# An encoder layer on one Trainium2 core: the sample in two blocks of 512 tokens, low weight parts kept in DRAM

## The chip, the cores and the metric

The kernel runs on one core of a Trainium2 chip. Its time is the device time of one execution in microseconds; less is better. The median of the runs stands for a kernel.

## The reference

One layer of a bidirectional hybrid encoder is applied, with the same weights, to a prompt of 512 tokens and to a sample of 1024 tokens, both 1024 channels wide, in float32.

```python
x = layer_norm(x, ln_in_g, ln_in_b)
h = x @ w_in                                   # 1024 -> 2048
c_val, c_gate, r_x, r_gate = split(h)          # 512 each
c = c_val * sigmoid(c_gate)
c = silu(layer_norm(conv31(c)))                # depthwise over tokens, width 31
rec = rg_lru(conv4(r_x), forward) + rg_lru(conv4(r_x), backward)   # gates 64x64, scan over all tokens
x = layer_norm(ALPHA * x + concat(c, rec * gelu(r_gate)) @ w_out)  # LN1
u = conv3(x @ w_up)                            # 1024 -> 5632, depthwise over tokens, width 3
val, gate = split(u)
x = layer_norm(ALPHA * x + (gelu(gate) * val) @ w_down)            # LN2
```

The scan of the recurrence goes over all tokens, once from the left and once from the right; the two convolutions of the sample reach 15 tokens and 1 token over any cut of it.

## The kernel before

**Products.** Every matrix operand is split in a high part (a copy rounded to f32r, line 236, ScalarE) and a low part (operand minus high part, line 197, VectorE or POOL), and a product is three matmuls of line 258: high x high, high x low, low x high. `weight` (lines 464 to 474) loads a raw weight tile of 128x1024 into a staging slot (ST0 to ST2), and `split` (lines 457 to 459) writes both parts into a weight slot. `lo_eng` names the engine of the low part; "any" leaves it to the scheduler, which takes the engine that would end first.

**The order.** All work is recorded as operations with priorities (a lower number goes first) and then put into a fixed order by a list scheduler (`emit`, line 270) with costs per engine. Each engine then runs its instructions in that order. All DMAs are issued from SyncE (SP), in one queue (line 247). Slots in SBUF and PSUM are given away by name; whoever takes a slot waits for its last user.

**The stages.** LN of the prompt; its w_in product; LN and w_in of the sample (its mixer inputs go to DRAM, `mixs_d`); the prompt's mixer (`mixer_p`, line 694), w_out and LN1 (`w_out_ln1`, line 727); the prompt's feed-forward (`ffn_p`, line 792); the sample's mixer (`mixer_s`, line 848), w_out and LN1 in two halves (line 912); the sample's feed-forward (`ffn_s`, line 928). While the prompt's feed-forward runs on TensorE, the sample's mixer, of lower priority, runs on VectorE, ScalarE and POOL, and its mixed channels go through DRAM (`xcat_d`) before w_out.

**The mixer.** For each of four channel blocks: `conv31` (line 629) has 30 taps, each a scalar_tensor_tensor on VectorE (line 206); each direction of the recurrence has `conv4` (three taps), a split, two gate products with sigmoids, `rg_decay` (line 659; exp, tanh and sqrt, each from another table of ScalarE) and `scan` (line 674). In `mixer_s` these are 1024 tokens wide, two directions for each of four blocks.

**The feed-forward.** The hidden width of 2816 is done in 22 pairs of 128 value and 128 gate channels. For a pair, two up tiles (24 matmuls for 512 tokens each, `mtile`, line 517), the width-3 convolution (`ffn_half`), gelu, a product and a split; then down products, in groups of pairs, are added to the residual. `ffn_p` has 512 tokens, three up slots (W0, W1, G3) and two down slots (A2, A3); `weight` there names POOL for the low parts. `ffn_s` has all 1024 tokens for each loaded weight.

**The end.** The last group of `ffn_s` has four pairs; as each of the eight 128-token tiles is complete, `ln2` (line 788) normalises and stores it.

## Time and profile before

| | us |
|---|---|
| runs (3), median | 1667.08 |
| runs, lowest and highest | 1663.58, 1668.41 |
| the profiled execution | 1662.43 |
| its span, first to last instruction | 1660.7 |
| busy: TensorE, VectorE, ScalarE, POOL | 1574.1, 1219.0, 721.0, 401.6 |
| DMA traffic | 152.35 MB, 27.7% of 16 engines |
| mean granted clock of TensorE | 0.979 |

In the profile a line is the line of a helper: 258 is every product, 266 every transpose, 236 every operation of ScalarE, 206 every scalar_tensor_tensor, 197 every two-tensor operation, 247 every DMA. Shapes tell the operations apart: 128x511 is a tap of the feed-forward's convolution, 128x1009 to 128x1023 taps of the sample's mixer, "128x1024 fp32r" a high or low part of a full weight tile.

### The profile page before, as it was taken

To read this page: it belongs to the slowest core of one execution; us is meant where nothing else is said; L and a number is where in the kernel's file an instruction comes from. 1 tells how busy PE (TensorE), PEld (TensorE's weight loads), DVE (VectorE), ACT (ScalarE), POOL (GpSimd) and SP (SyncE) were. 2 spreads that over 40 slices of the span, in tenths; PEclk is the share of its full clock that TensorE was granted. 3 is DMA by queue.
4 is the path that set the end of the run, shared out by engine and by line. 5 is a ranking of instruction groups with operands and counts; after the bars stand their busy time and mean duration, and the time that the engine had idled before them with its cause. 6 is when DMAs were issued, how large, how long until landed. Compare 5 with 4: busy or idle time off the path is not lost.

```text
span 1660.7 us, 17945 instructions
## 1 busy us (share of the span) xinstructions
PE 1574.1 (95%) x7008; PEld 1294.8 (78%) x7008; DVE 1219.0 (73%) x1608; ACT 721.0 (43%) x866; POOL 401.6 (24%) x230
## 2 busy tenths in 40 slices
PE   5999999999999999997899999999999999999995
PEld 5887777887877778776678788888888888888884
DVE  8999996999999998867776575555555555544548
ACT  3636767247957548586432422222232232221321
POOL 3123333136565456664120200000000000000006
PEclk9999999999999989999999999999999999999998
DMA  8632114243233233243742311111111111110102
GB/s 319 205 102 76 64 51 168 86 142 125 89 115 92 72 111 105 76 140 114 264 154 89 101 51 40 49 52 51 50 45 45 38 64 51 38 52 25 39 13 102
DMA packets 45877, 152.35 MB, mean 92 GB/s; under 512 B 5088, under 2 KB 5216, under 8 KB 45664
## 3 DMA queue, kind: packets, MB, share of 16 engines
q1 hardware_dynamic: 45792, 151.21, 27.7%
q8 instruction: 55, 0.90, 0.2%
q14 instruction: 30, 0.25, 0.0%
HBM read 128.12 MB, written 23.07 MB: 91 GB/s over the span
## 4 chain that ended last, share of the span: by engine, by line
PE 47%; DVE 3%; DMA 2%; ACT 1%; issue 1%; POOL 0%; SPq 0%; DVEq 0%; ACTq 0%
PE b L258 46%; DVE b L206 1%; DMA b<-xcat_d 1%; DVE b L197 1%; ACT b L236 1%; PE b L266 0%; DMA xcat_d<-b 0%; POOL b L197 0%; DVE b L413 0%; ACT L236 0%; DMA b<-w_up 0%; SPq L247 0%; DVE b L220 0%; DVE b L415 0%; DVEq L206 0%
## 5 line engine op out<-in xcount | busy, mean ns | idle before, releaser
L258 PE MATMUL b<-b,b 128*128 128x512 f32 (+1 forms) x6720 | 1546.2, 391 | 38.9 <-DVE b L197 20.1
L258 PEld LDWEIGHTS b<-b,b 128*128 128x128 f32 x6720 | 1260.7, 191 | 309.8 <-DVE b L197 28.4
L236 ACT ACTIVATE b<-b 128x1024 fp32r<-128x1024 f32 (+3 forms) x443 | 366.0, 850 | 678.1 <-PE b L258 422.1
L197 DVE TENSOR_TENSOR b<-b,b 128x512 f32<-128x512 f32 (+3 forms) x519 | 443.8, 874 | 264.4 <-ACT b L236 172.0
L206 DVE SCALAR_TENSOR_TENSOR b<-b,b,b 128x511 f32<-128x511 f32 (+20 forms) x668 | 557.8, 852 | 91.5 <-ACT b L236 79.4
L197 POOL TENSOR_TENSOR b<-b,b 128x1024 fp32r<-128x1024 f32 (+3 forms) x176 | 330.9, 1894 | 1157.2 <-DVE b L220 867.4
L236 ACT ACTIVATE b<-b,b 128x512 f32<-128x512 f32 (+2 forms) x330 | 251.4, 782 | 222.1 <-PE b L258 143.3
L236 ACT ACT_TABLE_LOAD x93 | 119.3, 1283 | 19.4 <-DVE b L206 17.2
L206 DVE SCALAR_TENSOR_TENSOR b<-b,b 128x512 f32<-128x512 f32 (+1 forms) x121 | 95.8, 807 | 25.9 <-PE b L258 13.5
L197 POOL TENSOR_TENSOR b<-b 128x512 f32<-128x512 f32 x46 | 70.8, 1543 | 95.2 <-ACT b L236 87.0
L413 DVE BATCH_NORM_STATS2 b<-b 128x6 f32<-128x512 f32 x84 | 57.0, 689 | 20.6 <-PE b L266 15.0
L266 PE MATMUL b<-b,b 128*128 128x128 f32 x288 | 42.2, 289 | 30.5 <-DVE b L206 12.8
L266 PEld LDWEIGHTS b<-b,b 128*128 128x128 f32 x288 | 35.3, 148 | 38.4 <-issue 12.2
L197 DVE TENSOR_TENSOR b<-b 128x1024 f32<-128x1024 f32 (+2 forms) x30 | 32.4, 1081 | 27.7 <-ACT b L236 27.4
L206 DVE SCALAR_TENSOR_TENSOR b<-b 128x1 f32<-128x1 f32 (+2 forms) x59 | 27.8, 474 | 3.5 <-POOL b L197 2.6
L677 DVE TENSOR_TENSOR_SCAN b<-b 128x512 f32<-128x512 f32 (+1 forms) x16 | 28.3, 1768 | 0.3
L220 DVE TENSOR_SCALAR b<-b 128x1 f32<-128x1 f32 (+1 forms) x61 | 10.2, 171 | 1.7
L415 DVE BATCH_NORM_AGGREGATE b<-b 128x2 f32<-128x12 f32 (+1 forms) x48 | 9.6, 199 | 1.0
masks.py:199 POOL TENSOR_SCALAR_AFFINE_SELECT b<-b 128x128 f32<-128x128 f32 x1 | 0.3, 292 | 0.1
L607 DVE RECIPROCAL b<-b 128x8 f32<-128x8 f32 x1 | 0.2, 204 | 0.0
L613 DVE RECIPROCAL b<-b 128x8 f32<-128x8 f32 x1 | 0.2, 203 | 0.0
masks.py:197 POOL MEMSET b<- 128x128 f32 x1 | 0.2, 204 | 0.0
(6 smaller groups left out, 0.6 us busy)
## 6 DMA issues: line engine op xcount, KB each, us to landing
b<-w_up SPq DMA_DIRECT2D x88, 512.0 KB, 3.7
b<-w_in SPq DMA_DIRECT2D x32, 512.0 KB, 3.8
b<-w_out SPq DMA_DIRECT2D x24, 512.0 KB, 4.2
b<-w_down SPq DMA_DIRECT2D x44, 256.0 KB, 3.1
b<-w_down SPq DMA_DIRECT2D x22, 512.0 KB, 3.6
mixs_d<-b SPq DMA_DIRECT2D x12, 512.0 KB, 2.6
b<-mixs_d SPq DMA_DIRECT2D x12, 512.0 KB, 3.5
b<-gb SPq DMA_DIRECT2D x10, 512.0 KB, 6.9
```

The lines of the kernel that those rows point to most:

```text
L197: return self.op(eng, cost if eng == "any" else cost[eng], lambda e=eng: self.engine(e).tensor_tensor(out=out(), in0=a(), in1=b(), op=op), ...
L206: o = self.op("dve", cost, lambda: self.nc.vector.scalar_tensor_tensor(out=out(), in0=a(), scalar=s() if isinstance(s, View) else s, in1=b ...
L220: return self.op(eng, cost, lambda: e.tensor_scalar(out=out(), in0=a(), scalar1=f(s1), scalar2=f(s2), op0=op0, **({"op1": op1} if op1 is n ...
L236: self.nc.scalar.activation(out=out(), in_=a(), func=func, **k)
L258: self.nc.tensor.matmul(out=out(), lhsT=a(), rhs=b(), start=start and i == 0, stop=stop and i == len(pairs) - 1)
L266: self.nc.tensor.transpose(o(), i(), ident())
L413: S.op("dve", c.n * 1.0417 + 69, lambda i=i, c=c: nc.vector.bn_stats(out=sm_[6 * i:6 * i + 6](), in_=c()), [c], [sm_[6 * i:6 * i + 6]], prio)
L415: S.op("dve", 211, lambda: nc.vector.bn_aggr(out=sm_[12:14](), in_=sm_[0:6 * n]().rearrange("p (a b) -> p a b", a=n)), [sm_[0:6 * n]], [sm ...
L607: S.op("dve", 150, lambda: nc.vector.reciprocal(out=d.all(), in_=c.all()), [c.all], [d.all], pr)
L613: S.op("dve", 150, lambda: nc.vector.reciprocal(out=d.all(), in_=c.all()), [c.all], [d.all], pr)
L677: S.op("dve", out.n * 2.0833 + 69, lambda: nc.vector.tensor_tensor_scan(out=out(), data0=a(), data1=b(), initial=0.0, op0=ALU.mult, op1=AL ...
```

## The change

The sample is cut in two blocks of 512 tokens, and the second block (tokens 512 to 1023, `blk` 1) goes first. The new sequence is: mixer of block 1 beside the prompt's feed-forward; w_out (`residual`) and LN1 (`ln1`) of block 1; mixer of block 0 beside the feed-forward of block 1; w_out and LN1 of block 0; feed-forward of block 0.

- The mixer of block 1 runs the forward recurrence over tokens 0 to 511 too (its output is kept in DRAM, `hf_d`) and carries its last state on; the first state of the backward scan is kept in `hbc`. So block 1 has three chains of 512 tokens per channel block, block 0 one. The mixed channels stay in SBUF (`xcf`); `xcat_d` is gone.
- One feed-forward function serves all three passes of 512 tokens. A weight's low part is computed in the prompt's pass, by "any" engine, and stored to DRAM (`lo_d`); the two later passes load raw tile and low part and compute the high part alone. The same holds for w_in and w_out.
- The last down group of a pass (four pairs, `last`) is recorded after the next block's `residual`, and has a later place on TensorE.
- Token 512 needs token 511, which is known only in the last pass: block 1 leaves its first token's hidden value zero; the pass of block 0 computes it (`f5`), multiplies each raw down tile by it on VectorE (`a5`), and a product with a one-column matrix (`E0`) sums it over partitions before the LN2 of tokens 512 to 639.

The core of the diff:

```diff
+    lo_d = {"in": tc.dram_tile([16, 128, 1024], F32, name="lo_in_d"),
+            "out": tc.dram_tile([8, 128, 1024], F32, name="lo_out_d"),
+            "up": tc.dram_tile([2 * NPAIR, 128, 1024], F32, name="lo_up_d"),
+            "down": tc.dram_tile([NPAIR, 128, 1024], F32, name="lo_down_d")}
+    k_lo = {}
+    raw_of = {}
+    def weight(slot, parts, prio, lo_eng="dve", hi_eng="act", st=None):
+        raw_of[id(w)] = t
+        if all((k, m, c.start) in k_lo for k, m, c, _ in pieces):
+            S.copy(hi_eng, w[0], t, prio)
+            for k, m, c, v in pieces:
+                S.load(v.f32, lo_d[k][m][:, c], prio, r=[k_lo[k, m, c.start]])
         else:
-            S.load(t, src, prio)
-        split(w[0], w[1], t, prio, hi_eng, lo_eng)
+            split(w[0], w[1], t, prio, hi_eng, lo_eng)
+            for k, m, c, v in pieces:
+                key = k_lo[k, m, c.start] = Dram()
+                S.dma(lambda k=k, m=m, c=c: lo_d[k][m][:, c], v.f32, v.n * 512, [v], [key], prio + 1)
...
+    def chain(rx, c, hl, d, j, t0, carry, bk, prio):
+        conv4(rx, lambda a, b: c[0, a:b], d, j, 512, prio, t0, N)
+        split(hl[0], hl[1], c[0], prio, lo_eng="pool")
+        rg_gates(c[0], (hl[0], hl[1]), c[1], d, j, bk, prio)
+        rg_decay(c[0], c[1], c[2], c[3], d, j, prio, "pool")
+        if carry is not None:
+            e = slice(0, 1) if d == 0 else slice(511, 512)
+            S.stt(c[0, e], c[1, e], carry, c[0, e], ALU.mult, ALU.add, prio)
+        scan(c[2], c[1], c[0], d, prio)
+    def mixer_s(blk, xslots, PC, PR):
+        t0 = 512 * blk
+        c0, c1 = (497, N) if blk else (0, 527)
+        xcf = [S.buf(n, [4, 512]) for n in xslots]
+        g = S.buf("G1", [2048])
+        acc = S.buf("G2", [4, 512])
+        ch = rot([S.buf(n, [4, 512]) for n in ("A4", "A5", "A7")])
+        hlb = S.buf("A6", [2, 2, 512], f32r)
+        hls = rot([(hlb[i, 0], hlb[i, 1]) for i in range(2)])
+        bk = rot(["M3", "C1"])
+        def conv(j):
+            S.load(g[1024:1024 + c1 - c0], s_d[j][:, c0:c1], PC, r=[k_s[j]])
+            pc = S.buf("C0", [512], psum=True)
+            conv31(lambda a, b: g[1024 + a - c0:1024 + b - c0], lambda a, b: pc[a:b], j, 512, PC, t0, N)
+            S.copy("act", acc[j], pc.all, PC)
+        def rec(j):
+            rn = N if blk else 515
+            S.load(g[0:rn], s_d[4 + j][:, 0:rn], PR, r=[k_s[4 + j]])
+            rx = lambda a, b: g[a:b]
+            if blk:
+                ca = ch()
+                chain(rx, ca, hls(), 0, j, 0, None, bk, PR)
+                S.dma(lambda j=j: hf_d[j], ca[2], 2 ** 18, [ca[2]], [k_hf[j]], PR)
+                cf = ch()
+                chain(rx, cf, hls(), 0, j, 512, ca[2, 511:512], bk, PR)
+                hf = cf[2]
+            else:
+                hf = None
+            cb = ch()
+            chain(rx, cb, hls(), 1, j, t0, None if blk else hbc[j:j + 1], bk, PR)
+            if blk:
+                S.copy("act", hbc[j:j + 1], cb[2, 0:1], PR)
+            else:
+                hf = cb[1]
+                S.load(hf, hf_d[j], PR, r=[k_hf[j]])
+            S.load(cb[3], s_d[8 + j][:, t0:t0 + 512], PR, r=[k_s[8 + j]])
+            S.tt("dve", cb[2], cb[2], hf, ALU.add, PR)
+            S.tt("dve", xcf[1][j], cb[2], cb[3], ALU.mult, PR)
+        for j in range(4):
+            rec(j)
+            conv(j)
+        nb = rot(["M3", "C1"])
+        for tt in range(4):
+            c = slice(tt * 128, (tt + 1) * 128)
+            conv_norm(lambda j: acc[j, c], [(0, 4, acc[:, c])], tt, "c", nb, PR)
+        for j in range(4):
+            b = S.buf(nb(), [512], psum=True)
+            S.transposes([(b[i * 128:(i + 1) * 128], acc[j, i * 128:(i + 1) * 128]) for i in range(4)], b.all, idn.all, PR)
+            S.act(xcf[0][j], b.all, AF.Silu, col(C_CG + j), col(C_CBB + j), PR)
+        return xcf
...
+    def split_block(xcf, prio):
+        xc = quads(["A4", "A5", "A6", "A7"])
+        for q in (1, 0):
+            for a in (slice(0, 2), slice(2, 4)):
+                split(xc[0][q][a], xc[1][q][a], xcf[q][a], prio, lo_eng="any")
+        return xc
+    GROUPS = [[0]] + [list(range(i, i + 3)) for i in range(1, 16, 3)] + [[16, 17], list(range(18, 22))]
...
+        if blk == 0:
+            a5 = S.buf("A4", [1024])
...
+        def up(p):
+            pr = PR + p * 0.01
+            for s in range(2):
+                m = s * NPAIR + p
+                w = weight(ws(), [("up", m, ALLC)], wprio, lo_eng="any")
+                u = ub()
+                mtile(w, x1, u.all, pr)
+                c = lambda k: col(C_FW + 3 * m + k)
+                v = va[p % 2, s]
+                acc = lambda a, b: va[p % 2, s, a:b]
+                S.act(v, u.all, AF.Identity, c(1), col(C_FB + m), ev)
+                S.stt(acc(1, 512), u[0:511], c(0), acc(1, 512), ALU.mult, ALU.add, ev)
+                S.stt(acc(0, 511), u[1:512], c(2), acc(0, 511), ALU.mult, ALU.add, ev)
+                if blk == 1:
+                    S.copy("dve", sv[m], u[0:2], ev)
+                if blk == 0:
+                    S.stt(acc(511, 512), sv[m, 0:1], c(2), acc(511, 512), ALU.mult, ALU.add, ev)
+                    S.stt(ex[p % 2, s:s + 1], u[511:512], c(0), ut[m:m + 1], ALU.mult, ALU.add, ev)
+            S.act(va[p % 2, 1], va[p % 2, 1], AF.Gelu_apprx_tanh, prio=ev)
+            if blk == 0:
+                S.act(ex[p % 2, 1:2], ex[p % 2, 1:2], AF.Gelu_apprx_tanh, prio=ev)
+                S.tt("dve", f5[p:p + 1], ex[p % 2, 0:1], ex[p % 2, 1:2], ALU.mult, ev)
+            r = slice(lo, 512)
+            S.tt("pool" if blk is None else "any", va[p % 2, 0, r], va[p % 2, 0, r], va[p % 2, 1, r], ALU.mult, ev)
+            f = fb[(p // 2) % 2]
+            split(f[p % 2, 0, r], f[p % 2, 1, r], va[p % 2, 0, r], ev, lo_eng="dve")
...
+                    w = weight(wdslot(), [("down", p_, slice(n_ * 512, (n_ + 1) * 512)) for n_, p_ in cs], wprio + 1,
+                               lo_eng="any")
+                    for i, ch_ in enumerate(cs):
+                        wd[ch_] = (w, i)
+                        if blk == 0:
+                            n_, p_ = ch_
+                            raw = raw_of[id(w)].buf[i * 512:(i + 1) * 512]
+                            o = a5[n_ * 512:(n_ + 1) * 512]
+                            if p_ == 0:
+                                S.ts("dve", o, raw, f5[p_:p_ + 1], ALU.mult, prio=wprio)
+                            else:
+                                S.stt(o, raw, f5[p_:p_ + 1], o, ALU.mult, ALU.add, wprio)
...
+            names = rot(["M2", "C0", "C1", "M3", "U3", "U0", "U1", "U2"])
+            nonlocal wdslot
+            wdslot = rot(["A2", "A3", "G2", "A5"])
+            up(NPAIR - 1)
+            get = wds(grp)
+            bank = {}
+            for i in range(2):
+                for nh in range(2):
+                    bank[nh, i] = S.buf(names(), [512], psum=True)
+                    S.mm(bank[nh, i].all, products(get, nh, i, grp[:-1]), True, False, pr)
...
+    WS = ["W0", "W1", "G3"]
+    xcf1 = mixer_s(1, ("T2", "T3"), 32, 31)
+    last_p = ffn(None, x1P, yP, 50.0, 6, 4)
+    xc1 = split_block(xcf1, 33)
+    y1 = [S.buf("T2", [2, D]), S.buf("T3", [2, D])]
+    UB = ["U3", "M2", "C0", "C1", "U0", "U1", "U2", "U3"]
+    residual(1, 1, xc1, y1, 40, UB, rot(WS), pe=50.2105)
+    last_p()
+    gb1a = load_gb("G2", 1, 36)
+    x1a = ln1(y1, gb1a, quads(["B0", "B1", "B2", "B3"]), "s", 37, rot(["M3", "C0"]), ["dve", "act"])
+    gb2a = load_gb("G1", 2, 40)
+    for i in range(4):
+        ln2(page_of(yP[i // 2], i % 2), gb2a, "p", 38, out_p[i * 128:(i + 1) * 128, :], "act")
+    xcf0 = mixer_s(0, ("T0", "T1"), 52, 51)
+    last_1 = ffn(1, x1a, y1, 60.0, 6, 44)
+    xc0 = split_block(xcf0, 53)
+    y0 = [S.buf("T0", [2, D]), S.buf("T1", [2, D])]
+    residual(1, 0, xc0, y0, 56, UB, rot(WS), pe=60.2105)
+    last_1()
+    gb1b = load_gb("G2", 1, 52)
+    x1b = ln1(y0, gb1b, quads(["B0", "B1", "B2", "B3"]), "s", 53, rot(["M3", "C0"]), ["dve", "act"])
+    gb2b = load_gb("G1", 2, 56)
+    for i in range(1, 4):
+        ln2(page_of(y1[i // 2], i % 2), gb2b, "s", 58, out_s[(4 + i) * 128:(5 + i) * 128, :], "act")
+    last_0 = ffn(0, x1b, y0, 70.0, 6, 64)
+    bank, get, grp, products = last_0()
+    E0 = S.buf("A6", [128], f32r)
+    S.op("pool", 200, lambda: nc.gpsimd.memset(E0.all.f32(), 0.0), [], [E0.all], 60)
+    S.op("pool", 100, lambda: nc.gpsimd.memset(E0[0:1].f32(), 1.0), [], [E0[0:1]], 60)
+    a5 = S.slots["A4"]
+    a5s = S.buf("A7", [2, 1024], f32r)
+    split(a5s[0], a5s[1], a5.all, 5)
+    for i in range(4):
+        for nh in range(2):
+            b = bank[nh, i]
+            S.mm(b.all, products(get, nh, i, grp[-1:] if i < 2 else grp), i >= 2, True, 70.21 + 0.01 * i)
+            yv = y0[i // 2][i % 2, nh * 512:(nh + 1) * 512]
+            S.tt("dve", yv, yv, b.all, ALU.add, 6)
+        if i == 1:
+            for nh in range(2):
+                b = S.buf("M2" if nh == 0 else "C0", [512], psum=True)
+                c = slice(nh * 512, (nh + 1) * 512)
+                S.mm(b.all, [(E0.all, a5s[0, c]), (E0.all, a5s[1, c])], True, True, 70.225)
+                yv = y1[0][0, c]
+                S.tt("dve", yv, yv, b.all, ALU.add, 7)
+            ln2(page_of(y1[0], 0), gb2b, "s", 46.9, out_s[512:640, :], "act", "pool")
+        ln2(page_of(y0[i // 2], i % 2), gb2b, "s", 46 + 0.5 * i, out_s[i * 128:(i + 1) * 128, :], "act" if i < 3 else "dve",
+            "pool" if i == 0 else "dve")
```

`conv31` and `conv4` take a first token and the sequence length as well; the old `w_out_ln1` is cut into `residual` and `ln1`; `ffn_p`, `ffn_s` and the old `mixer_s` are gone.

## Rows read from the trace of the kernel before

**Rows 1.** The page's part 1: busy us (share of the span) and instructions by engine

```profile
PE 1574.1 (95%) x7008; PEld 1294.8 (78%) x7008; DVE 1219.0 (73%) x1608; ACT 721.0 (43%) x866; POOL 401.6 (24%) x230
```

**Rows 2.** Windows by stage: length, busy us (instructions) by engine, clock, DMA share, GB/s

```profile
0.00:41.50 41.50, 24.64 (x173) 23.57 (x174) 35.07 (x52) 14.44 (x17) 15.90 (x19) 1.00 0.85 319
124.50:290.50 166.00, 157.28 (x683) 127.63 (x681) 148.84 (x200) 114.69 (x142) 53.52 (x30) 0.97 0.26 90
290.50:373.50 83.00, 83.00 (x383) 68.97 (x382) 78.50 (x85) 28.11 (x34) 19.08 (x11) 1.00 0.34 114
373.50:747.00 373.50, 352.67 (x1502) 285.00 (x1502) 334.27 (x363) 261.44 (x319) 221.25 (x112) 0.97 0.33 103
747.00:954.50 207.50, 184.64 (x813) 149.18 (x813) 144.57 (x203) 88.12 (x109) 48.50 (x33) 0.94 0.44 145
954.50:1618.50 664.00, 664.00 (x2931) 550.00 (x2930) 361.21 (x520) 166.24 (x184) 0.00 (x0) 1.00 0.15 44
```

**Rows 3.** The same windows, products of line 258 alone on TensorE

```profile
124.50:290.50 166.00, 154.76 (x651) 0.97 0.26 90
373.50:747.00 373.50, 351.00 (x1482) 0.97 0.33 103
747.00:954.50 207.50, 173.62 (x705) 0.94 0.44 145
1618.50:1660.00 41.50, 24.89 (x110) 0.83 0.25 102
```

**Rows 4.** Groups by line and shape, VectorE, 373 to 788 us

```profile
L206 DVE SCALAR_TENSOR_TENSOR b<-b,b,b 128x511 f32<-128x511 f32 x88 | 65.7, 747 | 15.0 <-ACT b L236 13.3
L206 DVE SCALAR_TENSOR_TENSOR b<-b,b 128x512 f32<-128x512 f32 x56 | 49.5, 906 | 10.2 <-ACT b L236 8.9 <-POOL b L197 1.1
L197 DVE TENSOR_TENSOR b<-b,b 128x512 fp32r<-128x512 f32 x24 | 23.8, 995 | 4.4 <-ACT b L236 4.4
L206 DVE SCALAR_TENSOR_TENSOR b<-b,b,b 128x1023 f32<-128x1023 f32 x14 | 22.1, 1580 | 0.1
L677 DVE TENSOR_TENSOR_SCAN b<-b 128x1024 f32<-128x1024 f32 x8 | 18.3, 2289 | 0.2
```

**Rows 5.** The same view, VectorE, 290 to 373 us

```profile
L206 DVE SCALAR_TENSOR_TENSOR b<-b,b 128x512 f32<-128x512 f32 x8 | 5.4, 677 | 0.0
L197 DVE TENSOR_TENSOR b<-b,b 128x512 fp32r<-128x512 f32 x8 | 5.2, 685 | 0.0
L206 DVE SCALAR_TENSOR_TENSOR b<-b,b,b 128x1023 f32<-128x1023 f32 x3 | 3.9, 1297 | 0.0
```

**Rows 6.** The same view, whole span: full-width low parts on POOL and VectorE

```profile
L197 POOL TENSOR_TENSOR b<-b,b 128x1024 fp32r<-128x1024 f32 x91 | 229.4, 2528 | 239.5 <-ACT b L236 195.4 <-issue 40.6 <-POOL b L197 2.0
L197 DVE TENSOR_TENSOR b<-b,b 128x1024 fp32r<-128x1024 f32 x121 | 152.0, 1263 | 153.2 <-ACT b L236 152.7
```

**Rows 7.** The same view, ScalarE, 373 to 788 us; then pieces of the chain

```profile
L236 ACT ACT_TABLE_LOAD x59 | 75.7, 1283 | 11.0 <-DVE b L206 10.1
L236 ACT ACTIVATE b<-b 128x1024 fp32r<-128x1024 f32 x63 | 65.7, 1054 | 44.6 <-PE b L258 20.4 <-DMA b<-w_up 14.6 <-issue 7.2
...
781.41 1.28 ACT L236
782.71 1.54 ACT b L236 x3
```

**Rows 8.** The page's part 6: DMA issues, KB, us to landing

```profile
b<-w_up SPq DMA_DIRECT2D x88, 512.0 KB, 3.7
b<-w_down SPq DMA_DIRECT2D x44, 256.0 KB, 3.1
```

**Rows 9.** Timeline of TensorE, 790 to 830 us: start, us, what, [idle before]

```profile
819.63 6.42 PE L258 MATMUL b<-b,b 128*128 128x512 f32 x20 [2.97 <-DVE b L197]
829.76 0.63 PE L258 MATMUL b<-b,b 128*128 128x512 f32 x1 [3.71 <-DVE b L197]
```

**Rows 10.** Groups by line and shape, VectorE, 1600 to 1661 us

```profile
L206 DVE SCALAR_TENSOR_TENSOR b<-b,b,b 128x1024 f32<-128x1024 f32 x8 | 17.2, 2162 | 0.3
```

More of the change, by code (lines that the diff above doesn't have):

```diff
@@ L820, in ffn_p @@
             pr = PR + (grp[-1] + 0.5) * 0.01
             for nh in range(2):
-                for c in range(0, len(chunks), 2):
-                    cs = chunks[c:c + 2]
-                    if cs[0] not in wd and cs[0][0] <= nh:
-                        w = weight(wdslot(), [w_down[p][:, n_ * 512:(n_ + 1) * 512] for n_, p in cs], 5,
-                                   lo_eng="any" if gi == len(groups) - 1 else "pool")
-                        for i, ch_ in enumerate(cs):
-                            wd[ch_] = (w, i)
```

360 lines of the change are left out of this document (118 added, 242 removed).

## Prediction

> **What bounds the kernel now.** I read the page's totals first, then the stretches, then who waits in the bad ones. TensorE is busy 95% of the span of 1660.7 us [rows 1], so the question is what its products cost at best and where more than that was spent. In the long last stretch, the feed-forward pass of the sample, TensorE never stops: 2931 products of 128x512 in 664.0 us, 226.5 ns each, at granted clock 1.00, the 2.4 GHz level [rows 2]. The change keeps every product, so only time above that rate can be won. I take loss of a stretch as its idle time plus the busy time of its products above 226.5 ns each:
> - 124.5 to 290.5 us (prompt mixer): idle 166.0 - 157.28 = 8.7; 651 products should take 147.5 and took 154.8, so 7.3; loss 16 [rows 2, 3].
> - 373.5 to 747 (prompt feed-forward beside the whole sample mixer, stage A below): idle 20.8; 1482 products should take 335.7 and took 351.0; loss 36.
> - 747 to 954.5 (end of the mixer, w_out, LN1 of the sample): idle 22.9; 705 products should take 159.7 and took 173.6; loss 37.
> - 954.5 to 1618.5: none. After it 110 products in 24.89 us put the last product at 1643.4, and 17 us follow, VectorE's backlog and a store [rows 3, 10].
> - At the start some 18 us before the first products run densely [rows 2].
>
> **Why stage A loses.** VectorE is busy 334 of 373.5 us there and POOL 221 [rows 2]. Operations of VectorE are longer beside POOL: the 1023-wide tap takes 1580 ns against 1297 in 290 to 373, where POOL is nearly quiet (19 of 83 us), and the low part of a 512-wide split 995 against 685 [rows 4, 5]. The order is fixed beforehand, mixer work fills every gap of VectorE, so each excess pushes the feed-forward's evictions behind it back, and TensorE waits. The granted clock is 0.97 in the stretch, partly at the 1.2 GHz level after such gaps.
>
> **The change, part by part.**
>
> *Stage A, VectorE.* Out: 82 of the 120 sample conv31 taps lie here, at some 1.28 us (105 us; the quiet price of the 1023-wide tap is 1.30 [rows 5]). Half the tokens at 512 wide need 120 taps of 0.75 us, the price of the 511-wide tap [rows 4]; of these some 63 fit before 373, where 37 wide ones lie now, so 57 x 0.75 = 43 remain: -62. The 8 wide recurrence chains cost some 14.8 us each (three conv4 taps near 1.5, two gate products 0.68, eight half-width steps 0.86, scan 2.29); the new stage has 12 narrow ones of 7.3: -30. Sums and normalisation halve: -8. In: every low part of the prompt's weights, so far named for POOL, becomes "any". What "any" means can be counted now: POOL did 91 full-width low parts, 87 of them explicitly its own, VectorE 121, of which 92 its own; so 29 of 33 free ones went to VectorE [rows 6]. Of 63 weights 55 move, x 1.22 us = +67. Shorter splits beside a quieter POOL: -6. Since records overlap slightly I scale by 0.95: 364 us (373 to 788) - 37 = 327, against some 376 us of products (1584 of the prompt, 72 for gates, a few transposes). POOL falls from 221 to about 70 us (22 products, 12 low parts, 12 decay products at 1.35 to 1.55 us). The excess of VectorE beside POOL, some 27 us (the 42 widest taps 0.16 to 0.30 us each, 24 low parts 0.31, 56 two-operand steps 0.906 - 0.677 = 0.23 [rows 4, 5]), falls with it to a third. I take the loss of stage A from 36 to 14: -22; ends -31 and -6 (VectorE remains packed and nothing tells me that the remaining excess does not sit on TensorE's path).
>
> *ScalarE in stage A.* Its work is 300 us now, of which 59 table loads are 75.7 [rows 7]. Twelve chains instead of eight and the same 22 gelu calls make perhaps 80 loads: 103 us; total some 330 of 410 us. It stays below TensorE's time. A load costs 1283 ns, and a function starts 0.02 us behind it (781.41 + 1.28, next at 782.71) [rows 7]. The Trainium skill ("ScalarE: Activation LUTs", What ACT_TABLE_LOAD costs) gives a switch about 1.38 us more for a drain and advises to batch by table set; this speaks against a mixer cut in blocks. By that price 80 loads would add 110 us, ScalarE would need 440 us and stage A would end some 30 us later, near 1671; the row shows no such drain, so it has 1 chance in 100, inside the late-mixer rival below.
>
> *Stores in stage A.* 66 stores of 512 KB are new in SP's queue. Each waits there for a low part, and the next raw loads are queued behind it, for which ScalarE's copies wait. Those loads need the staging slot that the same low part releases, so the store waits for nothing that SP didn't wait for before: 0, unless VectorE is late (then stage A's upper end, -6).
>
> *124.5 to 290.5.* Sixteen low parts of w_in, 2.5 us each on POOL [rows 6], become loads; 40 of POOL's 53 us vanish beside a VectorE that is busy 149 of 166 [rows 2]. Loss 16 to 12: -4 (0 to -8).
>
> *Start.* Sixteen stores of 512 KB join a stretch that moves 319 GB/s at a DMA share of 0.85 [rows 2]; the later load of w_in waits behind them in SP's order. 8.4 MB at 319 GB/s are 26 us of traffic, most of it due after 41.5, while 16 w_in tiles are being used up. +3 (0 to +8).
>
> *Transitions.* Now one: mixer end, a round trip of the mixed channels through DRAM, w_out, LN1, with gaps such as 2.97 and 3.71 us that end on the split of channels read back [rows 9]. The round trip goes. After: two transitions (A to B, B to C), each with w_out of one block (192 products, 43.5 us) put before the last four down pairs (96 products, 21.7 us), which cover LN1. VectorE's LN1 takes 4 x (two evictions' rest, statistics, two full-width steps, two low parts) = some 24 us from 3 us before w_out's end, with 4 us of latencies and 5 us of the eight last additions ahead of it by priority: about 29 us. Cover: 21.7, plus some 4 us for the third and fourth down weight, which wait for a slot. So idle 4 + 4 and some 4 at the lower clock: 12 each. 37 to 24: -13 (-25 to -5).
>
> *Stages B and C.* The sample's feed-forward runs twice at 512 columns, each weight in 5.4 us of products instead of 10.9. The high part is again ScalarE's, 1.05 us [rows 7]; the low part is a load, in three slots: 10.9 us from a slot's release to its need, against 3.7 us to landing for 512 KB [rows 8]. Per weight 1.05 MB in 5.4 us, 193 GB/s, below the 319 seen [rows 2]. 66 x 1.22 us of low parts leave VectorE; in C 44 multiplications for the boundary token come (0.8 us each, 35 us), at the lowest priority, hidden by TensorE's 359 us, since VectorE has some 130 us else there. B has four chains and half the taps (130 us of VectorE) beside it; by stage A's measure, a third of its mixer, I take +6 (+2 to +12); C +4 (0 to +12). If a cover fails, see the rivals.
>
> *Boundary.* Four products: +1. *Tail.* Five LN2 of tiles instead of seven or eight behind the last weights; VectorE's work there is 42 us now (16 additions, 16 statistics, eight full-width steps at 2.16, small ones [rows 10]); ten, ten and six of them with what the boundary adds are some 27. But TensorE's last products shrink as well, from 126 (29 us) to 64 (14.5 us). Behind the last product VectorE still has about 12 us and a store some 4.5: 17 now, 16 then: -1 (-3 to +3).
>
> **Sum.** -22 - 4 + 3 - 13 + 6 + 4 + 1 - 1 = -26, so a span of 1635. The profiled execution took 1662.4, 1.7 over its span, and the median of the three runs 1667.1 is 6.4 over that span; on the median's side I forecast **1641 us**, with 1629 to 1661 as its own range.
>
> **Rivals.**
> 1. *More is won:* the loss of A falls to 5, that of 124 to 290 to 8, the transitions to 12 together, B costs 2, C and the start nothing, the tail -3: -31 - 8 - 25 + 2 + 1 - 3 = -64, 1603 us. For it: TensorE ran 664 us without a gap when VectorE was at 54% [rows 2]. Against: VectorE at 87% in A.
> 2. *It doesn't do what it says:* low parts on VectorE take what the smaller mixer gave. A 30, transitions 20 + 12, start 3, 124 to 290 -2, rest as above: 0, 1667 us.
> 3. *The mixer of the second block comes late (slower).* It has the lowest priority on VectorE, and each of the 12 chains passes five engines. If its channels are ready more than 21.7 us after the last up product (near 751), the last down pairs have been used up as filler; then LN1 stands bare. Price: A to B 45 instead of 12 (15 waiting, 27 LN1, 3 clock), A 30: +25, 1692 us. For it: the mixer ends now in a stretch where VectorE is at 70% [rows 2], so on the length of its chains, and each chain has ScalarE's table loads in it [rows 7]. Against: three chain buffers, and 327 us of work for 400 us.
> 4. *Low parts land late (slower).* Down weights have two slots; the third of a group can be fetched only after the first is released. If no up product is ready, 3 us are lost in each of 16 such places of B and C: 48, so 1689 us. Against: 3.1 us for 256 KB [rows 8] and up products in hand.
>
> **Chances.** Forecast 0.43, rival 1 0.24, rival 2 0.13, rival 3 0.12, rival 4 0.08. The range reaches from rival 1 to rival 3, 1603 to 1692. A measurement of this kernel tells some 0.3% (5 us) from no change: faster 0.67, within 0.13, slower 0.20.
>
> **What would show it.** In stage A: POOL near 70 us, the taps at their short price, fewer waits for VectorE, a granted clock near 1.00. Between A and B, and B and C: gaps of 8 us or so, w_out's 192 products right behind the last up product; a long gap before w_out is rival 3. In B and C: 226 ns a product; gaps that end on a load of low parts are rival 4. About 310 MB moved. I am wrong if TensorE idles in B or C, or if ScalarE, not VectorE, ends most waits in A.

## The result and the profile after

The changed kernel takes 1618.39 us (median of four runs, 1616.81 to 1619.14) against 1667.74 us for the kernel before beside it (1663.58 to 1669.47): a ratio of 0.9706, 95% interval 0.9686 to 0.9726. It is faster by 49 us. The profiled execution has a span of 1615.0 us, 45.7 less than before. That lies inside the range of 1603 to 1692, but outside the forecast's own 1629 to 1661.

The page's part 1, busy time by engine, of the kernel after (of before: [rows 1]):

```profile
span 1615.0 us, 19015 instructions
PE 1556.7 (96%) x7012; PEld 1281.2 (79%) x7012; DVE 1200.4 (74%) x1867; ACT 820.3 (51%) x1019; POOL 188.1 (12%) x159
```

Windows of after by stage, with the columns of [rows 2]. The stages have other bounds now: 373.5 to 742 is stage A (w_out of block 1 starts at 742.01), 742 to 812 the way from A to B, 812 to 1163 stage B, 1163 to 1229 the way from B to C, then stage C.

```profile
0.00:41.50 41.50, 24.00 (x173) 22.93 (x174) 35.07 (x52) 14.45 (x17) 15.91 (x19) 1.00 0.95 361
124.50:290.50 166.00, 163.99 (x737) 134.99 (x736) 138.09 (x198) 114.65 (x142) 24.23 (x19) 1.00 0.41 140
373.50:742.00 368.50, 354.44 (x1536) 286.91 (x1534) 329.73 (x442) 251.66 (x308) 70.52 (x49) 0.99 0.60 194
742.00:812.00 70.00, 68.92 (x318) 56.93 (x319) 39.45 (x65) 22.24 (x26) 8.99 (x8) 1.00 0.59 196
812.00:1163.00 351.00, 348.10 (x1549) 287.32 (x1548) 266.25 (x433) 182.75 (x222) 19.32 (x24) 1.00 0.66 216
1163.00:1229.00 66.00, 63.84 (x294) 51.91 (x293) 33.88 (x58) 20.98 (x24) 4.45 (x6) 1.00 0.59 193
1229.00:1577.00 348.00, 345.85 (x1520) 284.17 (x1519) 183.48 (x349) 130.34 (x175) 11.81 (x10) 1.00 0.57 190
```

The same windows with the products of line 258 alone, as in [rows 3]:

```profile
124.50:290.50 166.00, 161.96 (x705) 1.00 0.41 140
373.50:742.00 368.50, 352.17 (x1504) 0.99 0.60 194
742.00:812.00 70.00, 66.21 (x286) 1.00 0.59 196
812.00:1163.00 351.00, 345.82 (x1517) 1.00 0.66 216
1163.00:1229.00 66.00, 61.37 (x264) 1.00 0.59 193
1229.00:1577.00 348.00, 345.61 (x1515) 1.00 0.57 190
```

Loss is worked out as in the prediction: idle time plus the products' time above 226.5 ns each. For 124.5 to 290.5 it is 166.0 - 163.99 = 2.0, and 161.96 - 705 x 0.2265 = 2.3, together 4.3.

| stretch | loss before | forecast | loss after |
|---|---|---|---|
| 124.5 to 290.5 | 16 | 12 | 4.3 |
| stage A | 36 | 14 | 25.6 |
| end of the mixer, w_out, LN1 (one before, two after) | 37 | 24 | 2.5 + 3.7 |
| stage B | 0 | 6 | 5.1 |
| stage C | 0 | 4 | 4.6 |
| from the last product to the end | 17 | 16 | 15.9 |

The way from A to B on TensorE (start, us, what, and in brackets the idle time before it with its releaser):

```profile
742.01 46.32 PE L258 MATMUL b<-b,b 128*128 128x512 f32 x203 [0.95 <-DMA b<-lo_out_d]
788.17 1.03 PE L266 MATMUL b<-b,b 128*128 128x128 f32 x8
798.49 1.06 PE L266 MATMUL b<-b,b 128*128 128x128 f32 x8 [0.19 <-DVE b L206]
800.67 8.23 PE L258 MATMUL b<-b,b 128*128 128x512 f32 x35 [0.88 <-DVE b L197]
808.74 1.03 PE L266 MATMUL b<-b,b 128*128 128x128 f32 x8
```

Where the kernel before had two gaps of 3 to 4 us [rows 9] and more like them, the longest here is 0.95. The transposes of LN1 lie between down products, the last of them at 808.74. From 742 to 1615 us the waits of TensorE (total us, times, longest) are as short; besides these two groups there is the 0.95 us on a low part of w_out above, and 0.5 us in two waits of the transposes:

```profile
PE b L258 <- DVE b L197: 5.9, 10, 1.4
PE b L258 <- DMA b<-lo_down_d: 1.7, 2, 1.1
```

VectorE's groups by shape in stage A (instructions | busy us, mean ns | idle before), to be read against [rows 4]:

```profile
L197 DVE TENSOR_TENSOR b<-b,b 128x1024 fp32r<-128x1024 f32 x59 | 74.7, 1277 | 19.6 <-ACT b L236 16.8 <-DMA lo_up_d<-b 2.1 <-DMA b<-w_down 0.3
L197 DVE TENSOR_TENSOR b<-b,b 128x512 f32<-128x512 f32 x63 | 42.1, 680 | 3.2 <-PE b L258 3.2
L206 DVE SCALAR_TENSOR_TENSOR b<-b,b,b 128x512 f32<-128x512 f32 x54 | 41.6, 773 | 1.2 <-ACT b L236 0.5
L206 DVE SCALAR_TENSOR_TENSOR b<-b 128x512 f32<-128x512 f32 x48 | 34.0, 721 | 0.3
```

### The profile page after: what moved, and what is told of

Read it like the earlier page. It is cut to its first block, busy times and chain, and to the rows that moved or that the text cites. A ratio compares the mean times of both kernels' runs of the same rounds, so it can differ in the third digit from the quotient of the medians.

```text
span 1615.0 us, 19015 instructions
## 1 busy us (share of the span) xinstructions
PE 1556.7 (96%) x7012; PEld 1281.2 (79%) x7012; DVE 1200.4 (74%) x1867; ACT 820.3 (51%) x1019; POOL 188.1 (12%) x159
## 4 chain that ended last, share of the span: by engine, by line
PE 50%; DVE 26%; ACT 10%; DMA 9%; issue 4%; SPq 0%; POOL 0%; DVEq 0%; ACTq 0%; POOLq 0%
PE b L258 48%; DVE b L206 15%; DVE b L197 9%; ACT b L236 7%; DMA b<-w_up 6%; ACT L236 3%; PE b L266 1%; DMA b<-mixs_d 1%; DMA b<-w_down 1%; DVE b L708 1%; DMA lo_in_d<-b 1%; DVE b L413 0%; DMA b<-lo_out_d 0%; DMA b<-xp 0%; SPq L247 0%
## 5 line engine op out<-in xcount | busy, mean ns | idle before, releaser
L258 PE MATMUL b<-b,b 128*128 128x512 f32 (+1 forms) x6724 | 1532.1, 389 | 24.5 <-DVE b L197 15.9
L206 DVE SCALAR_TENSOR_TENSOR b<-b,b,b 128x511 f32<-128x511 f32 (+12 forms) x848 | 593.0, 715 | 177.5 <-ACT b L236 156.6
L236 ACT ACTIVATE b<-b 128x1024 fp32r<-128x1024 f32 (+4 forms) x576 | 447.3, 799 | 533.6 <-PE b L258 197.2
L197 DVE TENSOR_TENSOR b<-b,b 128x512 f32<-128x512 f32 (+6 forms) x483 | 396.0, 840 | 122.8 <-ACT b L236 70.4
L236 ACT ACTIVATE b<-b,b 128x512 f32<-128x512 f32 (+1 forms) x337 | 256.9, 784 | 220.9 <-PE b L258 160.3
L197 POOL TENSOR_TENSOR b<-b,b 128x1 f32<-128x1 f32 (+3 forms) x89 | 113.6, 1282 | 674.1 <-DVE b L220 443.7
L236 ACT ACT_TABLE_LOAD x106 | 136.0, 1283 | 26.7 <-DVE b L206 23.9
L206 DVE SCALAR_TENSOR_TENSOR b<-b,b 128x512 f32<-128x512 f32 (+2 forms) x81 | 53.6, 673 | 62.5 <-PE b L258 61.8
L197 DVE TENSOR_TENSOR b<-b 128x512 f32<-128x512 f32 (+3 forms) x80 | 46.5, 600 | 25.8 <-ACT b L236 24.9
L206 DVE SCALAR_TENSOR_TENSOR b<-b 128x512 f32<-128x512 f32 (+1 forms) x110 | 56.0, 518 | 6.8 <-POOL b L197 3.4
L266 PEld LDWEIGHTS b<-b,b 128*128 128x128 f32 x288 | 34.8, 145 | 23.9 <-DVE b L206 10.7
L708 DVE TENSOR_TENSOR_SCAN b<-b 128x512 f32<-128x512 f32 x24 | 29.3, 1223 | 0.7
```

The source lines that it names most:

```text
L197: return self.op(eng, cost if eng == "any" else cost[eng], lambda e=eng: self.engine(e).tensor_tensor(out=out(), in0=a(), in1=b(), op=op), ...
L206: o = self.op("dve", cost, lambda: self.nc.vector.scalar_tensor_tensor(out=out(), in0=a(), scalar=s() if isinstance(s, View) else s, in1=b ...
L236: self.nc.scalar.activation(out=out(), in_=a(), func=func, **k)
L258: self.nc.tensor.matmul(out=out(), lhsT=a(), rhs=b(), start=start and i == 0, stop=stop and i == len(pairs) - 1)
L266: self.nc.tensor.transpose(o(), i(), ident())
L708: S.op("dve", out.n * 2.0833 + 69, lambda: nc.vector.tensor_tensor_scan(out=out(), data0=a(), data1=b(), initial=0.0, op0=ALU.mult, op1=AL ...
```

## The experiments

The order here goes by question. Ratios are to the kernel before, with 95% intervals. "Over after" is the difference of two ratios, times 1665 us; after itself has 0.9706.

**Is it the place of w_out?** e2 records the last down pairs before w_out, in both transitions:

```diff
-    residual(1, 1, xc1, y1, 40, UB, rot(WS), pe=50.2105)
     last_p()
+    residual(1, 1, xc1, y1, 40, UB, rot(WS), pe=50.22)
...
-    residual(1, 0, xc0, y0, 56, UB, rot(WS), pe=60.2105)
     last_1()
+    residual(1, 0, xc0, y0, 56, UB, rot(WS), pe=60.22)
```

> The changed kernel, but w_out of each sample block is put behind the last four down pairs of the pass before, not ahead of them. Theory (the last down pairs cover LN1): in the changed kernel w_out ends near 785.5 and the last transposes of LN1 start at 808.7, with 1.1 us of TensorE idle between; without the cover TensorE stands still for about 20 us in each of the two transitions and restarts at the 1.2 GHz level: +40 to +50 us over the changed kernel, some 1660 to 1668. Rival (the round trip of the mixed channels through DRAM was the cost, and the order doesn't matter): within 5 us of 1618.

1663.03 us, 0.9995 [0.9981, 1.0009]: 48 us over after, the whole gain. TensorE's timeline of e2 at the same place:

```profile
773.47 40.43 PE L258 MATMUL b<-b,b 128*128 128x512 f32 x177 [1.26 <-DVE b L197]
823.47 1.94 PE L266 MATMUL b<-b,b 128*128 128x128 f32 x8 [8.30 <-DVE b L197]
833.23 1.94 PE L266 MATMUL b<-b,b 128*128 128x128 f32 x8 [5.42 <-DVE b L197]
```

With nothing left to multiply, LN1 stands bare: 8.30 and 5.42 us between its transposes. From 742 to 880 us TensorE idles 20.8 us at a granted clock of 0.93, and from 1163 to 1300 us 19.0, also at 0.93. Without this order a kernel with two transitions pays for both; with it both are nearly free.

**Is it w_in's low parts on POOL?** e3 neither stores nor loads those of w_in, so POOL computes them again for the sample; e7 puts them, and nothing else of the change, into the kernel before; e10 keeps in DRAM only those of w_in; e1 keeps none.

```diff
+                if k == "in":
+                    continue
                 key = k_lo[k, m, c.start] = Dram()
```

> The changed kernel, but the sample's w_in tiles have their low parts computed on POOL again, as before the change, and the low parts of w_in are neither stored nor loaded. Theory (operations of VectorE are longer beside POOL, and this is what TensorE lost in 124.5 to 290.5 us): the loss there goes back from 4 to about 16, taps of 509 to 511 from 750 ns to 830 to 930, and the kernel takes +8 to +12 us, 1626 to 1630. Rival (the gain there comes from elsewhere, such as staging slots that come free earlier for other reasons): within 3 us of 1618; if the stores at the start cost, faster by up to 3.

1636.39, 0.9837 [0.9812, 0.9862]: 22 us over after, more than either figure. The stretch of the prompt's mixer in e3, all engines, and then two of VectorE's groups there:

```profile
124.50:290.50 166.00, 152.69 (x665) 123.55 (x664) 150.24 (x198) 112.06 (x140) 52.88 (x31) 0.98 0.22 74
```

```profile
L206 DVE SCALAR_TENSOR_TENSOR b<-b,b 128x512 f32<-128x512 f32 x24 | 24.1, 1022 | 2.2 <-ACT b L236 2.1
L710 DVE TENSOR_TENSOR_SCAN b<-b 128x512 f32<-128x512 f32 x8 | 11.9, 1489 | 0.1
```

In after the same 24 steps take 827 ns and the 8 scans 1223. With 12 long low parts of POOL in the stretch (one in after) VectorE's 198 instructions take 12 us more, and TensorE lost 13.3 us of idle time in place of 2.0, at clock 0.98. It does 665 instructions there in place of 737, 72 less (16 us at 226.5 ns each), and from 373.5 to 742 us 1506 in place of 1536 (7 us); that makes up the 22. Of the 13.3 us, 7.5 end on VectorE, 3.1 on ScalarE and 2.7 on POOL's own low parts (in after 2.0, all on VectorE). So e3 shows that low parts on POOL cost this time, but not that VectorE's longer operations are the only way.

The edit of e7 (the stores go to a tensor of sixteen tiles, as in the change; its declaration, `weight`'s new argument `m_in` and the three calls that pass it are left out here):

```diff
...
-        split(w[0], w[1], t, prio, hi_eng, lo_eng)
+        if m_in in k_lo:
+            S.copy(hi_eng, w[0], t, prio)
+            S.load(w[1].f32, lo_d[m_in], prio, r=[k_lo[m_in]])
+        else:
+            split(w[0], w[1], t, prio, hi_eng, lo_eng)
+            if m_in is not None:
+                key = k_lo[m_in] = Dram()
+                S.dma(lambda m=m_in: lo_d[m], w[1].f32, w[1].n * 512, [w[1]], [key], prio + 1)
...
```

> The kernel before with one part of the change alone: the low parts of w_in are stored to DRAM by the prompt and loaded by the sample; all else as before. Theory (POOL's 40 us beside VectorE cost the loss of 124.5 to 290.5): the loss there goes from 16 to about 5, and the kernel takes 8 to 12 us less, 1655 to 1659. Rival (the later stages wait for something else anyway, or the stores cost at the start): within 3 us of 1667.

1658.04, 0.9955 [0.9933, 0.9976]: 7.5 us won, where e3 priced the same loads at 22. Windows of e7, with the bounds of [rows 2]:

```profile
124.50:290.50 166.00, 162.32 (x728) 133.18 (x727) 158.00 (x216) 115.98 (x144) 25.06 (x19) 1.00 0.40 136
373.50:747.00 373.50, 339.98 (x1448) 272.85 (x1447) 333.67 (x345) 261.83 (x316) 212.43 (x108) 0.97 0.31 99
747.00:954.50 207.50, 190.16 (x848) 153.98 (x847) 148.29 (x210) 90.89 (x114) 47.23 (x31) 0.96 0.43 145
```

Against [rows 2] TensorE does 728 instructions instead of 683 in the first stretch, and 1448 instead of 1502 in stage A: 45 gained, 54 given back. What comes earlier into an unchanged stage A, with POOL at 212 us, is lost there again. From 747 to 954.5 us it does 848 in place of 813, and these 35 are where e7 comes out ahead.

The edit of e10 is that of e3 with the condition turned round (`k != "in"`).

> The changed kernel with low parts in DRAM for w_in alone; those of w_out, up and down tiles are computed in every pass by 'any' engine. Undoing w_in alone cost 22 us and undoing all 23, so theory: low parts of the feed-forward in DRAM are worth about nothing (0 to 3 us), 1616 to 1622, although VectorE in stage B is near 99% busy. The theory from before the runs (a packed VectorE loses 15 to 20 us in B): 1633 to 1640. If the stores in stage A cost: faster than 1618 by up to 5.

1620.45, 0.9724 [0.9699, 0.9749]: 3 us over after, within the noise. So the low parts of w_up, w_down and w_out in DRAM, 74 of the 90 tiles that are stored, bring 0 to 3 us. Windows of e10:

```profile
373.50:742.00 368.50, 358.60 (x1558) 291.33 (x1557) 334.08 (x443) 248.88 (x306) 72.61 (x50) 0.99 0.34 108
812.00:1163.00 351.00, 344.56 (x1519) 280.96 (x1518) 318.83 (x478) 181.61 (x220) 47.19 (x27) 1.00 0.37 119
```

Without the stores stage A is 22 instructions of TensorE ahead of after (some 5 us), and stage B, where VectorE computes them again and is busy 319 of 351 us, 30 behind (some 7). VectorE at 91% leaves TensorE 6.4 us idle there in place of 2.9, so most of that work is off TensorE's path.

The edit of e1:

```diff
-                key = k_lo[k, m, c.start] = Dram()
-                S.dma(lambda k=k, m=m, c=c: lo_d[k][m][:, c], v.f32, v.n * 512, [v], [key], prio + 1)
+                pass
```

> The changed kernel without low parts in DRAM: every pass computes them ('any' engine in the feed-forward and w_out, POOL in the sample's w_in), nothing is stored or loaded. Theory: VectorE gets some 80 us more in each of stages B and C; B (266 us busy of 351) becomes as packed as stage A and loses 15 to 20 us, C (183 of 348) up to 5, and 124.5 to 290.5 loses its 10 as well: 1645 to 1655. Rival (the doubled DMA traffic and SP's longer queue cost as much as VectorE gains): within 5 us of 1618, with a lower loss in stage A since 66 stores are gone.

1637.85, 0.9847 [0.9815, 0.9879]: 23 us over after, no more than e3 alone. What costs is w_in, not the feed-forward's 66 weights.

**Is it "any" in place of POOL?** e4 names POOL for the low parts of the prompt's feed-forward, as before; e6 gives "any" to the kernel before.

```diff
-                    w = weight(ws(), [("up", m, ALLC)], wprio, lo_eng="any")
+                    w = weight(ws(), [("up", m, ALLC)], wprio, lo_eng="pool" if blk is None else "any")
...
-                               lo_eng="any")
+                               lo_eng="pool" if blk is None and grp[-1] < NPAIR - 1 else "any")
```

> The changed kernel, but in the prompt's pass POOL is named for the low parts of the weights, as before the change ('any' had put nearly all on VectorE). VectorE is rid of some 70 us in stage A, POOL has some 150 us more. Theory (what counts is VectorE's lengthening beside POOL): the loss of stage A goes up from 26 to 30 to 36, so 1622 to 1628. Rival (what counts is how much VectorE has to do): the loss falls to about 15, so 1607 to 1610.

1638.04, 0.9843 [0.982, 0.9867]: 23 us over after; the direction is that of the lengthening theory, the size more than twice its figure. From e4, 373.5 to 725 us: all engines, then TensorE's costliest waits in stage A, then five of VectorE's groups.

```profile
373.50:725.00 351.50, 316.77 (x1354) 255.89 (x1354) 297.19 (x362) 234.56 (x287) 195.39 (x99) 0.96 0.57 182
```

```profile
PE b L258 <- DVE b L206: 23.8, 3, 9.8
```

```profile
L206 DVE SCALAR_TENSOR_TENSOR b<-b 128x512 f32<-128x512 f32 x48 | 53.0, 1116 | 3.6 <-ACT b L236 3.5
L197 DVE TENSOR_TENSOR b<-b,b 128x512 f32<-128x512 f32 x56 | 38.7, 700 | 11.8 <-PE b L258 11.0 <-ACT b L236 0.6
L708 DVE TENSOR_TENSOR_SCAN b<-b 128x512 f32<-128x512 f32 x12 | 20.0, 1665 | 0.2
L206 DVE SCALAR_TENSOR_TENSOR b<-b,b,b 128x510 f32<-128x510 f32 x10 | 14.7, 1474 | 0.2
L206 DVE SCALAR_TENSOR_TENSOR b<-b,b,b 128x507 f32<-128x507 f32 x3 | 2.2, 748 | 0.1
```

VectorE has less to do than in after (297 against 320 us) and TensorE does 111 instructions less. The steps of the recurrence chains (the x48 group) went from 721 to 1116 ns and the scans from 1222 to 1665, but the additions that empty a bank of PSUM only from 680 to 700: an operation with one input in PSUM hardly notices POOL. The taps say the same: widths 497 to 508 belong to `conv31` alone, whose sum lies in a bank of PSUM (`pc`), and keep 731 to 748 ns, while the group of 510, which holds `conv4`'s taps with both inputs in SBUF as well, means 1474. The Trainium skill (GPSIMD Engine Reference, Specifications) says that POOL shares its SBUF interfaces with VectorE and contends with its operations that have two SBUF inputs; the rows agree, and give the sizes.

How it reaches TensorE is the line of 23.8 us: three waits, 9.8 us the longest, on line 206. Here is the first of them in TensorE's timeline, and then VectorE's groups in the 11 us before its end (424.5 to 435.85):

```profile
435.99 23.98 PE L258 MATMUL b<-b,b 128*128 128x512 f32 x96 [6.84 <-DVE b L206]
```

```profile
L206 DVE SCALAR_TENSOR_TENSOR b<-b,b,b 128x511 f32<-128x511 f32 x5 | 3.7, 744 | 0.1
L206 DVE SCALAR_TENSOR_TENSOR b<-b,b,b 128x510 f32<-128x510 f32 x1 | 2.8, 2833 | 0.0
L206 DVE SCALAR_TENSOR_TENSOR b<-b 128x512 f32<-128x512 f32 x2 | 2.4, 1200 | 0.0
```

The last two instructions that end before the wait does, and so before each of the three, are 511 wide: by their place the two taps of the feed-forward's own convolution, which read an up product out of its bank. VectorE was never idle; it had mixer work ahead of them in its fixed order, among it a tap of 0.75 us that took 2.83. So a mixer operation that POOL holds up delays a bank that TensorE needs, though the mixer's results are needed only much later. The sizes fit: in the 30 us before the three waits end, VectorE never pauses for 0.1 us, and its steps, taps and scans take 6.7, 6.9 and 9.1 us more than at their quiet prices (an estimate, with 0.72 us for what is 512 wide, 0.75 for the narrower taps and 1.22 for a scan), beside waits of 6.84, 7.17 and 9.82. What is not shown apart is the order: an edit of this kind makes the scheduler set another one, and in e7, with POOL as busy as before (212 against 221 us), such waits on line 206 in stage A are 14.9 us in four, against 2.8 in one in the kernel before.

The edit of e6, in the kernel before:

```diff
-                w = weight(ws(), w_up[m], 4, lo_eng="pool")
+                w = weight(ws(), w_up[m], 4, lo_eng="any")
...
-                           lo_eng="any" if gi == len(groups) - 1 else "pool")
+                           lo_eng="any")
```

> The kernel before with one part of the change alone: low parts of the prompt's feed-forward weights on 'any' engine instead of POOL. VectorE gets some 67 us more in stage A (364 busy of 415 before), POOL some 150 less. Theory of load: the mixer ends later, so +10 to +25 us, 1677 to 1692. Theory of lengthening (VectorE's operations become shorter beside a quiet POOL, and low parts are ready sooner): within 5 us of 1667, or faster by up to 10.

1683.44, 1.0107 [1.0092, 1.0122]: 18 us slower than before. Windows of e6:

```profile
373.50:747.00 373.50, 365.25 (x1584) 296.60 (x1583) 364.46 (x400) 276.56 (x330) 77.78 (x52) 1.00 0.34 107
747.00:954.50 207.50, 155.10 (x664) 121.33 (x664) 154.80 (x218) 74.18 (x97) 47.86 (x34) 0.84 0.38 130
```

Stage A is nearly cured (1584 instructions against 1502, clock 1.00), with VectorE full (364 of 373.5); the mixer of 1024 tokens is then not done, and behind it 149 instructions are missing. So the same edit costs 18 us with the large mixer and is worth 23 with the smaller one. This is the third rival's mechanism.

**The cut without its two helpers.** e9 takes e1 and e2 together: two blocks, with "any" in the prompt's pass as in the change, but no low parts in DRAM and no covered LN1.

> What is left of the change when both its helpers are undone: the sample in two blocks, but no low parts in DRAM (each pass computes them) and w_out of a block behind the last down pairs. If the two effects seen so far, +48 us for the order and +23 us for the low parts, simply add: 1685 to 1692, so 1.1 to 1.5% slower than the kernel before. If they overlap (a later mixer or a more packed VectorE hides in the bare LN1): 1665 to 1680.

1681.69, 1.0091 [1.0063, 1.012]: slower than before, 64 us over after, where e1 and e2 give 23 + 48 = 71. The cut wins nothing by itself, even with "any" beside it. It makes room for "any" and lets a w_out have products behind it. The cut with POOL named as before was not run.

**What keeps 25.6 us in stage A?** Four runs. e5 leaves taps out:

```diff
-            if d == 0:
+            if d == 0 or (N == NS_TOK and d % 2):
                 continue
```

> The changed kernel without the taps at odd distances of the sample's conv31 (16 of 30 taps of each channel block are left out, so the conv's result is another). VectorE is rid of some 45 us in each of stages A and B. Theory (stage A loses because low-priority mixer work keeps VectorE packed): the loss of A falls from 26 to 10 to 14, B from 5 to 2, 1600 to 1606. Rival (A loses through ScalarE, late loads of raw weights, or SP's queue): A stays at 22 to 26, 1615 to 1618.

1613.25, 0.9685 [0.9669, 0.9702]: only 3.5 us below after, though VectorE falls from 320 to 288 us between 373.5 and 725; the loss there is 24.2 us, against 23.9. The load of VectorE alone is not what keeps the loss.

e8 gives the down products a third bank of PSUM and the mixer one in place of two:

```diff
-        bk = rot(["M3", "C1"])
+        bk = rot(["M3"])
...
-        nb = rot(["M3", "C1"])
+        nb = rot(["M3"])
...
-        st = {"db": rot([S.buf(n, [512], psum=True) for n in ("U3", "M2")])}
+        st = {"db": rot([S.buf(n, [512], psum=True) for n in ("U3", "M2", "C1")])}
```

> The changed kernel, but the down products of all three passes rotate over three PSUM banks (U3, M2, C1), and the block mixers have one bank (M3) for gates and transposes instead of two. Several of TensorE's short waits in stage A end on a 512-wide addition of VectorE, the one that empties a down bank. Theory (two down banks are what is left of the loss in stage A): A falls from 26 to about 15 and B and C by 1 to 2 each, 1602 to 1608. Rival (the gates' second bank is worth as much, or the waits move to another operation of VectorE): 1614 to 1622.

1620.91, 0.9734 [0.9709, 0.976]: no gain. TensorE idles 20.2 us in stage A in place of 14.1; 7.9 of them end on ScalarE (2.6 in after), which reads the mixer's one bank, and the waits on VectorE's additions are 7.7 in place of 8.1. So a third bank for the down products takes nothing from the waits it was meant for; what it would do without the bank taken from the mixer is not shown.

e11 takes the rest of POOL's work beside the mixer to VectorE (its last line also binds the gate's product of the two later passes), and e12 does that without the odd taps:

```diff
-        split(hl[0], hl[1], c[0], prio, lo_eng="pool")
+        split(hl[0], hl[1], c[0], prio, lo_eng="dve")
...
-        rg_decay(c[0], c[1], c[2], c[3], d, j, prio, "pool")
+        rg_decay(c[0], c[1], c[2], c[3], d, j, prio, "dve")
...
-            S.tt("pool" if blk is None else "any", va[p % 2, 0, r], va[p % 2, 0, r], va[p % 2, 1, r], ALU.mult, ev)
+            S.tt("dve", va[p % 2, 0, r], va[p % 2, 0, r], va[p % 2, 1, r], ALU.mult, ev)
```

> The kernel after, with the work that GpSimd still does beside the mixer given to VectorE: the split of a low part and the decay's product in the mixer's chain, and the product of value and gate of the feed-forward pass. Theory (VectorE's two-operand steps lengthen while GpSimd works, and the gate products and evictions of TensorE wait for them; GpSimd's 70.5 us in the overlapped stage are what is left of that): the steps of VectorE beside the mixer get shorter though there are more of them, the stage's idle time falls, 1608 to 1614 us. Rival (what is left of that stage's loss is the load of VectorE itself, 330 of 368 us, which now rises): no gain, 1616 to 1624 us, with longer waits of TensorE on VectorE.

1634.55, 0.9821 [0.9799, 0.9843]: 19 us over after. e11 up to 725 us, then its timeline of TensorE:

```profile
373.50:725.00 351.50, 341.98 (x1483) 277.26 (x1482) 331.73 (x448) 236.26 (x290) 6.52 (x2) 1.00 0.59 190
```

```profile
743.49 1.33 PE L266 MATMUL b<-b,b 128*128 128x128 f32 x5 [11.14 <-ACT b L236]
758.09 48.35 PE L258 MATMUL b<-b,b 128*128 128x512 f32 x204 [1.81 <-ACT b L236]
```

Both theories hold, at different places. Up to 725 us the loss is 15.6 us, against 23.9 in after by the same view (338.37 us busy, VectorE 320, POOL 69), and 46 products more are done. But the transposes of the mixer's normalisation then wait 11.14 us and more for their inputs, and w_out starts at 758.09 in place of 742.01: the lead of 10 us is lost, and 16 more.

> e11_no_pool and e5_half_taps together: GpSimd's work beside the mixer on VectorE, and the taps of the sample's 31-wide convolution at odd distances left out (the result is then another). Theory (in e11 TensorE loses 8 us less before 725 us, because GpSimd no longer lengthens VectorE's steps, and all of that and more is lost again when the mixer ends 16 us late, VectorE having too much to do): without the taps the mixer is ready in time, and the gain stays, 8 us below e5: 1603 to 1608 us. Rival (what e11 lost less before 725 us is only work that its late mixer pushed behind it, and GpSimd's part costs nothing): as e5, 1611 to 1617 us.

1601.38, 0.9616 [0.96, 0.9633]: 11.5 us below e5, even below the range given. From 373.5 to 725 us, first e12 and then e5:

```profile
373.50:725.00 351.50, 345.01 (x1515) 280.34 (x1516) 307.29 (x426) 244.58 (x302) 6.98 (x6) 1.00 0.62 200
```

```profile
373.50:725.00 351.50, 337.12 (x1468) 273.84 (x1468) 288.20 (x373) 235.59 (x291) 65.63 (x47) 0.99 0.61 194
```

VectorE does 19 us more and TensorE loses 13.1 us instead of 24.2. So, without the odd taps, about half of what stage A still loses goes with the 60 us of POOL's work; it can't be had by moving that work to VectorE while all 30 taps are there, since the mixer then comes late. The other half stays open. Open too is by which way POOL costs it: the chain steps shrink from 860 ns in e5 to 686 in e12 (48 of them, 8 us), but POOL's own longer operations go at the same time. No exact version tried beats the kernel after.

## Why the prediction was right in sign and 23 us off in size

- **The bound and the yardstick** held: TensorE busy 96%, four more products, and the terms measured by loss add up. 10.4 + 11.7 + 30.8 - 0.6 - 5.1 - 4.6 + 1.1 - 1 (boundary) = 42.7 of the 45.7 us, where the forecast had 26. Of the other 3, some 2 are the transposes of line 266, which loss leaves out (42.15 us busy before, 40.04 after); the medians are 3.7 further apart than the spans.
- **Transitions: the term that failed most** (-13 forecast, -31 measured). The step was "about 29 us. Cover: 21.7, plus some 4 us". LN1 ran from w_out's end (742.01 + 192 x 0.2265 = 785.5) to its last transposes at 808.74: 23 us, not 29. Its own transposes (4 us) add to the cover, and the third and fourth down weight cost 0 to 1.7 us instead of 4. So 23 us lie behind 26 us of products, next to nothing idles, and the clock stays at 1.00. Three terms of 4 us were each priced singly; together they were 2.5 and 3.7 us in place of 12 and 12.
- **124.5 to 290.5: too small** (-4 forecast, -12 measured). POOL fell from 53.5 to 24.2 us (29 us vanished where 40 should have). The step that failed is the worth of it, which the prediction set at a quarter of the loss: with the low parts back on POOL (e3) VectorE is busy 12 us more there and TensorE idles 11 us more, 5.5 of them in waits on VectorE, 3.1 on ScalarE and 2.7 on POOL itself. In the kernel before the same edit is worth 7.5 us (e7): its stage A gives the lead back, and only what follows it gains.
- **Stage A: too large** (-22 forecast, -10 measured). The loads of the engines were right: VectorE 330 us (327 forecast), POOL 70.5 (70), clock 0.99, the taps of 511 at 758 ns and of 509 and 510 at 847 and 857. The excess of VectorE beside POOL also fell as forecast: against e12's prices (749 and 686 ns, 1220 for the low part) 54 x 0.024 + 48 x 0.035 + 59 x 0.057 = 6.3 us, and 2 more for the taps of 509 and 510, of some 27 before. The step that failed was to let the loss of TensorE fall with it in proportion. It fell by less than a third; e12, without the odd taps, wins back about half of what is left, and the rest stays open. The 1580 ns that the prediction took for the 1023-wide tap are a mean of two kinds, six taps of `conv31` and eight of `conv4`; widths of `conv31` alone kept 1267 to 1285 beside the same POOL, so `conv4`'s were near 1.8 us, an estimate: (22.1 - 6 x 1.28) / 8.
- **ScalarE**: 51 table loads in stage A, not 80, and 252 us, not 330; more calls shared a table than I took it. A load is 1283 ns, in after too. That this would not hurt was right.
- **Stores and loads**: forecast at 0 in stage A. They cost some 5 us there at most (e10), part of it as VectorE's low parts waiting for a slot whose store was still in flight (2.1 us in the group above), and give that back in B. Rival 4's places were there and cost 1.7 us in all.
- **Start** +0.6 (forecast +3), **B** +5.1 (+6), **C** +4.6 (+4), **tail** -1.1 (-1): right. The start moved 361 GB/s at a DMA share of 0.95, so the stores found room above the 319 of [rows 2].
- **The rivals.** "More is won" came closest: its sum with A at -10 instead of -31 is -43, as measured. Its two large terms besides A went further than it said (transitions 6.2 instead of 12, the prompt's mixer 4.3 instead of 8), its small ones less far. The forecast's two errors, 26 us too little and 12 too much, hid each other in part. The third rival did not happen (w_out begins 0.95 us after the last product), but e6 and e11 show it at work; its own terms, 33 and 16 on top of the forecast's -26, make +23 and 1690 us, not +25 and 1692.
